# A router's products with the weights held in the array and the turned tokens moving, in a two-layer transformer kernel on one Trainium2 core

## Chip, cores and metric

The kernel runs on one core of a Trainium2 chip. The metric is the device time of one execution in microseconds (us). The core has a matrix engine (TensorE; PE in the profile, with its weight loads shown apart as PEld), a vector engine (DVE), a scalar engine (ACT), a general engine (POOL), and a queue processor (SP) that mainly issues transfers from memory. Each engine runs its own queue of instructions in order; engines wait for each other by semaphores.

## What is computed

The reference is a trunk of two layers over 512 latent tokens and 256 context tokens, 1024 channels wide. Each layer mixes tokens (layer 0 by a Fourier transform and a short gated convolution, layer 1 by windowed attention), adds the result to the stream, and then sends each token to two of 32 experts. The part that matters here is the step between the two: the residual sum, the normed and modulated row, and the router's logits.

```python
xl = xl + g1_l * yl
hl2 = modulate(rms_norm(xl, norm_ffn_g[layer]), sh2_l, sc2_l).reshape(B * L, D)
...
xr = xf.astype(jnp.float32)
g_logits = xr @ w_rg.astype(jnp.float32) + b_rg.astype(jnp.float32)
g_prob = jax.nn.softmax(g_logits, axis=-1)
g_val, g_idx = lax.top_k(g_prob, 1)
e_logits = (xr @ w_re.astype(jnp.float32) + b_re.astype(jnp.float32)).reshape(
    T, N_GROUPS, EXPERTS_PER_GROUP)
```

There are 4 group logits and 32 expert logits, so the router is a product of 1024 channels by 36 columns for each token. In layer 0 both streams pass through it (768 tokens, six tiles of 128), in layer 1 only the latent one (four tiles).

## The kernel before

`mixer_out` (line 1478) is the end of a layer's mixer and the start of its expert stage. It makes the mixer's output projection in two halves of 512 columns, `hf` = 0 and 1. For each half it goes over the token tiles `m`; the generator `tile(m)` issues for one tile 24 products into one accumulator `ps` (name A in the profile, two buffers): eight channel blocks `j` with three products each (L1540). Then DVE multiplies the accumulator by the gate (L1544) and adds it to the residual tile `x1[m]` (L1545). In the first half each `tile(m)` is run through at once.

In the second half, `x1[m]` is complete after L1545, and the generator `rows_and_logits` (line 174) does the rest for that tile. Its first step turns the tile, eight 128 x 128 transposes into two accumulators (L193), which ACT copies to `hT` (L194). ACT also squares the row and sums it (L201, then the root L160); DVE works out the scale `r` in small steps (L158 to L168). In layer 0, POOL multiplies the tile by its norm gain (L203), and DVE finishes the row (L218), which goes to memory for the expert stage's gather. In layer 1, ACT and DVE write the row as two parts (L208, L211) instead. The second step is the router: eight products in f32 with a block of `hT` (128 channels by 128 tokens) stationary and 36 columns of router weights `ws` moving (L223), and one DVE instruction that scales by `r` and adds the constant row (L224). `ws` is made once for each stream by `router(s)` (line 1485), as the router's weights times the modulation.

The steps of two tiles are interleaved by hand. Each pass `m` of the loop first issues four channel blocks of tile `m`, then the first step of tile `m - 1`, then the other four blocks and the update of tile `m`, then one step of any routing group under way, then the router of tile `m - 1`. `in_order` chains PE's and DVE's instructions in just this order, so neither engine can pass over one that waits. ACT, POOL and SP have an order that the compiler's own scheduler chooses.

Routing groups (`Route.tiles`, line 308) work on two tiles at a time (`CUTS`): after the logits of a group, DVE finds the top group and the two experts (L329 to L348), PE ranks the tokens (L356), DVE makes one-hot rows (L358 to L366), and PE counts the slots (L288). After the last tile, the group of the last two tiles ends the routing, and the expert stage (`moe`) begins: in layer 0 with a gather of rows (L764), in layer 1 with products on rows that are still on the core. Expert weights are loaded through a ring of eight buffers (L748); some of these buffers are those of the mixer's output weights and come free with the last L1540.

The accumulators of turning, router and ranking share one name, B, with three buffers taken in turn (`psB`). In the attention stage of layer 1, L2021 makes eight products in f32 with 64 stationary columns each, written to the upper and the lower half of the partitions by turns, with 128 columns moving.

Of the kernel before, what the change touches and what calls it, by code (L numbers as in the profile page):

```python
# [85 lines left out]
def body(tc, I, out, upto=None, dbg=None):  # L86
# [60 lines left out]
    epst = stat.tile([128, 1], F32, name="epst")  # L147
    V.memset(epst, EPS)
    rsq = stat.tile([128, 2, 4], F32, name="rsq")

    def slot(i, shape, dt=F32):

# [21 lines left out]
    def rows_and_logits(m, xm, hq, a2, b2, ws, crow, route, h2dst, wk, psum):  # L174
# [43 lines left out]
            V.scalar_tensor_tensor(h2, h2, r, b2, op0=ALU.mult, op1=ALU.add)  # L218
            route.wrote = (S if last else G).dma_start(h2dst[m * 128:(m + 1) * 128, :], h2)
        yield  # L220
        p = psum([128, 36])
        for k in range(8):
            T.matmul(p, hT[:, k, :], ws[:, k, :], start=k == 0, stop=k == 7)  # L223
        V.scalar_tensor_tensor(route.lg[:, m, :], p, r, crow, op0=ALU.mult, op1=ALU.add)  # L224
        yield

# [1251 lines left out]
    def mixer_out(layer, NT, lhs, raws, whls, x1, psA, psB, hq, rq, mk_route, h2dst, mdp, rw=None):  # L1478
# [6 lines left out]
        def router(s):  # L1485

            md = mds[s]
            V.scalar_tensor_tensor(md[:, 1, :], md[:, 1, :], 1.0, gf, op0=ALU.add, op1=ALU.mult)
            ws[s] = rq.tile([128, 8, 36], F32, name=f"ws{s}")
            V.tensor_mul(ws[s], wr, md[:, 1, :, None].to_broadcast([128, 8, 36]))  # L1490
            p = psB([128, 36])
            for k in range(8):
                T.matmul(p, md[:, 0, k:k + 1].to_broadcast([128, 128]), wr[:, k, :], start=k == 0, stop=k == 7)
            crow[s] = rq.tile([128, 36], F32, name=f"cr{s}")
            V.tensor_add(crow[s], p, br)
# [7 lines left out]
        for hf in range(2):  # L1503
# [6 lines left out]
            def tile(m):  # L1510
# [23 lines left out]
                        next(rl[m])  # L1534
                ps = psA([128, 512])
                for j in range(8):
                    if j == 4:
                        yield
                    for i, (a, b) in enumerate(((0, 0), (1, 0), (0, 1))):
                        T.matmul(ps, lhs(m, a, j), whl[b][:, j, :], start=j == 0 and i == 0, stop=j == 7 and i == 2)  # L1540
# [15 lines left out]
            for m in range(NT):  # L1556

                with in_order(*((PE, DVE) if m else (PE,)), chain=chain):
                    t = tile(m)
                    next(t)  # L1560
                    if m > 0:
                        next(rl[m - 1])
                    next(t)
                    going = [g for g in going if next(g, 0) is None]
                    if m > 0:
                        next(rl[m - 1])
                    for a, b in zip(cuts, cuts[1:]):
                        if b == m:
                            going.append(route.tiles(a, b))
                            next(going[-1])  # L1570
# [557 lines left out]
```

## Time and profile before

| | |
|---|---|
| time, median of 3 runs | 1613.04 us (1612.2 to 1615.1) |
| the profiled execution | 1612.01 us, span 1610.2 us |
| mean granted clock of TensorE in it | 0.98 |
| memory traffic over the span | 313 GB/s in the mean |
| layer 0's router (second half of `mixer_out`) | from about 266 to 320 us |
| layer 1's router | from about 1096 to 1130 us |

A time line of the profile gives the start of a group of instructions in us from the span's start, its length in us, the engine, the line of the kernel, the operation, the tile written and the tiles read, the shapes and the count. In square brackets stands how long the engine was idle before, and what ended that wait. A line of an answer for one source line gives the shortest, middle and longest duration in ns. PE's durations include the way through the array, so neighbouring instructions overlap; what a block of work takes is read from the start of its first weight load to the start of the next block's.

### The profile page before, as it was taken

To read this page: it belongs to the slowest core of one execution; us is meant where nothing else is said; L and a number is where in the kernel's file an instruction comes from. 1 tells how busy PE (TensorE), PEld (TensorE's weight loads), DVE (VectorE), ACT (ScalarE), POOL (GpSimd) and SP (SyncE) were. 2 spreads that over 40 slices of the span, in tenths; PEclk is the share of its full clock that TensorE was granted. 3 is DMA by queue.
4 is the path that set the end of the run, shared out by engine and by line. 5 is a ranking of instruction groups with operands and counts; after the bars stand their busy time and mean duration, and the time that the engine had idled before them with its cause. 6 is when DMAs were issued, how large, how long until landed. Compare 5 with 4: busy or idle time off the path is not lost. (4 is left out here: it accounts for less than half of the span.)

```text
span 1610.2 us, 21863 instructions
## 1 busy us (share of the span) xinstructions
PE 1511.0 (94%) x8201; PEld 865.1 (54%) x8201; DVE 749.6 (47%) x1688; ACT 437.1 (27%) x877; POOL 147.8 (9%) x169
## 2 busy tenths in 40 slices
PE   5999999999998999999989989999999999789887
PEld 3777888843443444444447776668443454334332
DVE  3555764973335334333466975645622233122223
ACT  4321320311111010111047577644221122112110
POOL 2612310300000000000033210000000000000000
PEclk9999999999999999999989999999999999899989
DMA  9889673879999999999930121025989999999996
GB/s 383 301 331 347 228 259 107 294 298 425 424 424 425 373 425 423 425 424 425 385 123 1 53 53 53 1 63 174 398 363 426 426 427 426 427 427 426 427 426 261
DMA packets 105889, 503.57 MB, mean 313 GB/s; under 512 B 15860, under 2 KB 30772, under 8 KB 53808
## 3 DMA queue, kind: packets, MB, share of 16 engines
q1 hardware_dynamic: 90256, 446.60, 68.7%
q0 software_dynamic: 12352, 52.31, 8.6%
q10 hardware_dynamic: 3168, 3.17, 0.6%
q8 instruction: 68, 1.11, 0.3%
q14 instruction: 45, 0.37, 0.1%
HBM read 499.30 MB, written 5.32 MB: 313 GB/s over the span
## 5 line engine op out<-in xcount | busy, mean ns | idle before, releaser
L913 PE MATMUL p<-w,xt 128*64 128x512 f32 (+1 forms) x1040 | 334.7, 603 | 15.8 <-DMA w<-in_w_dram 15.5
L913 PE MATMUL p<-r,xt 128*64 128x512 f32 (+1 forms) x784 | 278.8, 603 | 10.2 <-issue 6.3
L850 DVE TENSOR_TENSOR x<-x,cp 128x512 f32<-128x512 f32 x224 | 148.3, 686 | 98.9 <-PE cp L849 98.8
L930 DVE TENSOR_TENSOR sg<-sg,p 128x512 f32<-128x512 f32 x29 | 20.0, 688 | 342.8 <-PE p L913 332.7
L913 PEld LDWEIGHTS p<-w,xt 128*64 128x64 f32 (+1 forms) x1040 | 99.8, 133 | 147.2 <-issue 117.3
L849 PE MATMUL cp<-y,ot 128*128 128x512 f32 x600 | 168.1, 417 | 6.3 <-DVE x L850 3.8
L1000 PE MATMUL yp<-w,ht 128*64 128x512 f32 (+1 forms) x496 | 157.7, 595 | 2.6 <-DMA w<-in_w_dram 2.0
L913 PEld LDWEIGHTS p<-r,xt 128*64 128x64 f32 (+1 forms) x784 | 84.3, 135 | 134.7 <-issue 125.3
L1000 PE MATMUL yp<-r,ht 128*64 128x512 f32 (+1 forms) x368 | 129.1, 596 | 1.7 <-DMA r<-in_w_dram 1.7
L849 PEld LDWEIGHTS cp<-y,ot 128*128 128x128 f32 x600 | 104.4, 191 | 45.9 <-DVE x L850 24.2
L836 ACT CAST y<-yp 128x512 fp32r<-128x512 f32 x56 | 32.9, 587 | 286.7 <-DVE yp L827 200.2
L1000 PEld LDWEIGHTS yp<-r,ht 128*64 128x64 f32 (+1 forms) x368 | 37.6, 133 | 67.4 <-issue 63.3
L1000 PEld LDWEIGHTS yp<-w,ht 128*64 128x64 f32 (+1 forms) x496 | 45.7, 132 | 46.3 <-issue 40.2
L1951 DVE CUSTOM_DVE_ANT_0 A<-A,band,nsink 128x640 f32<-128x640 f32 (+1 forms) x56 | 45.3, 831 | 34.1 <-PE A L1947 33.9
L913 PE MATMUL p<-hhi,xt 128*64 128x512 f32 (+1 forms) x112 | 52.4, 613 | 6.5 <-DMA hhi<-in_w_dram 6.3
L920 ACT ACTIVATE sg<-p 128x512 f32<-128x512 f32 x29 | 17.3, 598 | 139.9 <-PE p L913 139.9
L825 DVE SCALAR_TENSOR_TENSOR sg<-yp,gsc,r 128x512 f32<-128x512 f32 x30 | 22.4, 747 | 69.8 <-PE yp L1000 69.7
L764 POOL DMA_INDIRECT r<-h_d,gi x17 | 17.0, 999 | 410.2 <-PE tp L799 290.3
L834 DVE SCALAR_TENSOR_TENSOR yp<-yp,gs,grow 128x512 f32<-128x512 f32 x24 | 18.2, 759 | 78.1 <-PE yp L1000 76.7
L913 PE MATMUL p<-hlo,xt 128*64 128x512 f32 (+1 forms) x112 | 51.2, 605 | 3.5 <-DMA hlo<-in_w_dram 3.5
L1947 PEld LDWEIGHTS A<-kS,w 128*128 128x128 f32 x288 | 36.1, 188 | 24.7 <-ACT w L1997 12.7
L1953 ACT ACTIVATE P<-A,nm 128x640 f32<-128x640 f32 (+1 forms) x56 | 42.5, 759 | 25.4 <-DVE nm L1951 25.4
(558 smaller groups left out, 2680.8 us busy)
## 6 DMA issues: line engine op xcount, KB each, us to landing
w<-in_w_dram SPq DMA_DIRECT2D x190, 1024.0 KB, 19.5
r<-in_w_dram SPq DMA_DIRECT2D x144, 1024.0 KB, 19.4
w<-in_w_mod_dram POOLq DMA_DIRECT2D x12, 2048.0 KB, 9.8
hhi<-in_w_dram SPq DMA_DIRECT2D x23, 1024.0 KB, 19.6
hlo<-in_w_dram SPq DMA_DIRECT2D x23, 1024.0 KB, 19.6
mw<-in_w_mod_dram POOLq DMA_DIRECT2D x32, 512.0 KB, 6.9
w<-in_w_in_even_dram SPq DMA_DIRECT2D x13, 512.0 KB, 7.4
w<-in_w_mod_dram SPq DMA_DIRECT2D x3, 2048.0 KB, 12.4
```

The source lines that it names most:

```text
L825: V.scalar_tensor_tensor(yc, ys, near["gsc"][:, j:j + 1], near["grow"][1][:, hs], op0=ALU.mult, op1=ALU.mult)
L834: V.scalar_tensor_tensor(ys, ys, tb["gs"][:, j:j + 1], near["grow"][0][:, hs], op0=ALU.mult, op1=ALU.mult)
L836: hi = S.copy(Yr[j, hf][0], ys)
L849: T.matmul(p, ot if len(Yr[j, hf]) > 1 else ot.bitcast(F32), y, start=n == 0 and i == 0, stop=n == len(js) - 1 and y is Yr[j, hf][-1])
L850: return V.tensor_add(xs, xs, p)
L913: T.matmul(ps[rs], X[b][:, q, rs], W[j, wn, ab][:, q, :], start=q == 0, stop=q == 7)
L920: si = S.activation(H[b], ps[:, cs], AF.Silu)
L930: V.tensor_mul(H[b], H[b], P1[b])
L1000: T.matmul(py_[hf][rs, :], HT[b][:, q, rs], W[j, "w2", ab][:, q, hf * 512:hf * 512 + 512], start=q == 0, stop=q == 3)
L1947: T.matmul(ps[:, o0:o0 + w], qS[G_][:, c, b * 128:(b + 1) * 128], kS[part][:, 2 * G_ + c // 4, k0:k0 + w], start=part == 0, stop=part == 1)
L1951: V.tensor_tensor_reduce(out=ps[:, 0:w], in0=ps[:, 0:w], in1=bnd, op0=ALU.add, op1=ALU.min, scale=1.0, scalar=nsink[:, hd:hd + 1], accum_o ...
L1953: S.activation(P[:, 0:w], ps[:, 0:w], AF.Exp, bias=nm[:, c:c + 1], scale=-1.0, accum_out=ls[:, c:c + 1])
```

## The change

For every tile but the last of a layer, the router's products swap their operands: a block of 64 router columns (36 and 28 zeros) is stationary, and the 128 turned tokens move. Even channel blocks write the lower half of an accumulator of 128 partitions, odd ones the upper half. ACT copies that accumulator to `lt`, and one more product, with `lt` stationary and a matrix `fold` of two stacked unit blocks moving, adds the two halves and turns the result back to tokens by 36 columns. L224 then reads it as before. The last tile keeps the old products.

The order changes too. `tile(m)` of the second half pauses before channel blocks 3 and 5 instead of before 4, and `rows_and_logits` has one step more. A pass now issues three channel blocks, the first step of tile `m - 1`, two blocks, the new router and its copy, three blocks and the update, the routing group's step, and then the fold and L224.

```diff
+    fold = stat.tile([128, 64], F32, name="fold")[:, 0:36]
+    V.tensor_add(fold, ident[:, 0:36], ident[:, 64:100])
...
         yield
-        p = psum([128, 36])
-        for k in range(8):
-            T.matmul(p, hT[:, k, :], ws[:, k, :], start=k == 0, stop=k == 7)
+        if last:
+            p = psum([128, 36])
+            for k in range(8):
+                T.matmul(p, hT[:, k, :], ws[:, k, 0:36], start=k == 0, stop=k == 7)
+        else:
+
+            p = psum([128, 128])
+            for k in range(8):
+                a = k % 2 * 64
+                T.matmul(p[a:a + 64], ws[:, k, :], hT[:, k, :], start=k < 2, stop=k > 5)
+            lt = wk.tile([128, 128], F32, name="lt")
+            S.copy(lt, p)
+            yield
+            p = psum([128, 36])
+            T.matmul(p, lt, fold, start=True, stop=True)
         V.scalar_tensor_tensor(route.lg[:, m, :], p, r, crow, op0=ALU.mult, op1=ALU.add)
         yield
...
-            ws[s] = rq.tile([128, 8, 36], F32, name=f"ws{s}")
-            V.tensor_mul(ws[s], wr, md[:, 1, :, None].to_broadcast([128, 8, 36]))
+            ws[s] = rq.tile([128, 8, 64], F32, name=f"ws{s}")
+            G.memset(ws[s][:, :, 36:64], 0.0)
+            V.tensor_mul(ws[s][:, :, 0:36], wr, md[:, 1, :, None].to_broadcast([128, 8, 36]))
...
                 for j in range(8):
-                    if j == 4:
+                    if hf and j in (3, 5):
                         yield
...
                     t = tile(m)
+                    next(t)
+                    if m > 0:
+                        next(rl[m - 1])
                     next(t)
                     if m > 0:
                         next(rl[m - 1])
```

## The prediction

> **What bounds the kernel now.** I read the page first, then the answers for the old router line and for the nearest row to its new form, then the weight loads and all engines in order of time around both routers, then stretches of the span.
>
> ```profile
> span 1610.2 us, 21863 instructions
> PE 1511.0 (94%) x8201; PEld 865.1 (54%) x8201; DVE 749.6 (47%) x1688; ACT 437.1 (27%) x877; POOL 147.8 (9%) x169
> ```
> ```profile
> 288.30:314.60 26.30, 25.44 (x160) 21.62 (x159) 24.93 (x75) 7.85 (x17) 11.72 (x9) 1.00 0.79 269
> 316.00:322.00 6.00, 6.00 (x36) 5.26 (x36) 4.92 (x24) 2.08 (x5) 0.00 (x0) 0.50 1.02 393
> 324.50:330.00 5.50, 5.25 (x57) 4.40 (x55) 5.00 (x33) 0.28 (x2) 1.09 (x1) 1.00 0.01 5
> 345.00:765.00 420.00, 411.73 (x2072) 180.75 (x2070) 167.57 (x315) 50.97 (x90) 14.88 (x15) 0.99 1.00 420
> 1210.00:1590.00 380.00, 343.53 (x1792) 151.62 (x1785) 96.91 (x157) 72.57 (x152) 0.00 (x0) 0.97 1.01 425
> ```
>
> The page says 94% PE, but that is a mean over stages. The second fence gives stretches: length, then busy time of PE, PEld, DVE, ACT and POOL, the clock, the DMA share, GB/s. The two long stretches (the experts) are bound by DMA, at 420 and 425 GB/s. Just before the first one DMA moves 5 GB/s: it waits for the routing. So a router that ends earlier or later moves what follows by as much. In layer 0's router (288.30 to 314.60) PE is busy for 25.44 us of 26.30, but DVE for 24.93: both are full, and the question is which of them ends last.
>
> **What an edit costs on PE.**
>
> ```profile
> L223 PEld LDWEIGHTS B<-ws,hT x160: 186/192/338, 278.0 to 1129.7; 128*128 128x128 f32 x160
> ```
> ```profile
> 274.31 1.10 PEld L193 LDWEIGHTS B<-cst,x 128*128 128x128 f32 x8
> 275.32 2.62 PEld L1540 LDWEIGHTS A<-r,r 128*128 128x128 f32 x12
> 277.98 1.98 PEld L223 LDWEIGHTS B<-ws,hT 128*128 128x128 f32 x16
> 279.88 2.60 PEld L1540 LDWEIGHTS A<-r,r 128*128 128x128 f32 x12
> ...
> 286.19 1.98 PEld L223 LDWEIGHTS B<-ws,hT 128*128 128x128 f32 x16
> ...
> 966.47 0.85 PEld L2021 LDWEIGHTS B<-cst,es 128*64 128x64 f32 x16 [0.17 <-issue]
> 967.50 0.77 PEld L1947 LDWEIGHTS A<-kS,w 128*128 128x128 f32 x6 [0.17 <-ACT w L1997]
> ```
>
> From start to start, which leaves no overlap to be counted twice: the turn of a tile (L193) takes 275.32 - 274.31 = 1.01 us, twelve products of L1540 (four channel blocks) 277.98 - 275.32 = 2.66, so one block 0.665; a tile's router 279.88 - 277.98 = 1.90. That router is 16 weight loads for eight products (160 over ten tiles), so one product costs 0.24. Its new form, 64 stationary columns in alternating halves with 128 columns moving in f32, is what L2021 already does with 16 loads: 967.50 - 966.47 = 1.03, or 1.20 with the 0.17 that stood idle before it. I take 1.03. The fold is one product of the old form, 0.24. A tile's period on PE therefore goes from 8 x 0.665 + 1.01 + 1.90 = 8.23 (the rows give 286.19 - 277.98 = 8.21) to 5.32 + 1.01 + 1.03 + 0.24 = 7.60. It saves **0.63** a tile, 5.0 for the five tiles of layer 0 and the three of layer 1.
>
> [...]
>
> **What the order costs, layer 0.** The new router comes before the last three channel blocks of the next tile, so these end 5.32 + 1.01 + 1.03 = 7.36 after the period's start, where they ended 5.32 + 1.01 = 6.33 after it. Only they release the residual update L1544 and L1545, and all of DVE's later work is queued behind it.
>
> ```profile
> 286.61 0.70 DVE L1544 TENSOR_TENSOR A<-A,gr 128x512 f32<-128x512 f32 x1 [0.94 <-PE A L1540]
> 287.35 0.69 DVE L1545 TENSOR_TENSOR x<-x,A 128x512 f32<-128x512 f32 x1
> ...
> 288.32 0.25 DVE L224 SCALAR_TENSOR_TENSOR w<-B,rq,cr 128x36 f32<-128x36 f32 x1 [0.29 <-PE B L223]
> ...
> 289.30 2.39 POOL L203 TENSOR_TENSOR h<-x,a 128x1024 f32<-128x1024 f32 x1 [2.76 <-ACT h L201]
> ...
> 289.59 2.13 DVE L337 TENSOR_TENSOR w<-w 128x8 f32<-128x8 f32 x1
> ...
> 297.41 1.06 ACT L201 ACTIVATE h<-x 128x1024 f32<-128x1024 f32 x1 [4.72 <-DVE x L1545]
> ...
> 298.81 2.37 DVE L366 TENSOR_TENSOR w<-w 128x32 bf16<-128x32 bf16 x1
> ...
> 301.10 0.24 DVE L224 SCALAR_TENSOR_TENSOR w<-B,rq,cr 128x36 f32<-128x36 f32 x1
> ...
> 304.11 0.69 DVE L1544 TENSOR_TENSOR A<-A,gr 128x512 f32<-128x512 f32 x1
> ...
> 313.88 0.69 DVE L1545 TENSOR_TENSOR x<-x,A 128x512 f32<-128x512 f32 x1
> ...
> 314.64 1.17 PEld L193 LDWEIGHTS B<-cst,x 128*128 128x128 f32 x8 [1.02 <-PE B L223]
> 316.41 3.49 PEld L223 LDWEIGHTS B<-ws,hT 128*128 128x128 f32 x16
> ```
>
> Tile 1's products start at 274.31 - 2.66 = 271.65. Tile 2's blocks ended at 286.19, when the router started; now they end at 271.65 + 7.60 + 7.36 = 286.61, **0.42 later**: one saving is behind them, one earlier router is ahead. L1544 followed PE by 0.42 and does so again. The 0.29 wait of L224 goes, since the fold is done by 286.9; but a DVE operation of 64 elements (L337) stands still until POOL's multiplication, which starts from the updated tile, ends at 289.30 + 2.39. That end moves by 0.42 too, so the 0.29 is lost again in that stall. From there to 314.57 DVE has no room: what PE saves on tiles 2 to 4 buys nothing, and the last tile's turn, which today waits 1.02 for its update, waits longer.
>
> One more wait is added. The tile B has three buffers, taken in turn; with the fold's accumulator the order is turn, turn, router, (rank), fold, and the router's buffer is always that of the fold before it, which L224 must have read. For tile 3 its turn waits for the tile's update, at 297.4 + 0.4, then 1.01 and two blocks, 1.33: PE is at the router at 300.1. L224 of tile 2 ends at 301.10 + 0.24 + 0.42 = 301.8. Behind the waiting router stand the three blocks: router to 302.8, blocks to 304.8, L1544 at 305.2 where it was 304.11. So from here DVE is **1.1 later**, not 0.42. If the buffer doesn't bind, 0.42 stays, and if L337 falls clear of POOL, 0.1. Layer 0: +1.1 (0.1 to 1.6).
>
> **Layer 1.** Here DVE has room, and PE sets the end.
>
> ```profile
> 1104.22 1.09 PEld L193 LDWEIGHTS B<-cst,x 128*128 128x128 f32 x8
> 1104.48 1.28 ACT L160 ACT_TABLE_LOAD   x1
> 1105.97 1.05 ACT L194 COPY hT<-B 128x512 f32<-128x512 f32 x2
> ...
> 1113.82 1.16 ACT L208 ACTIVATE x<-x,rq 128x1024 fp32r<-128x1024 f32 x1
> ...
> 1124.70 1.86 PEld L223 LDWEIGHTS B<-ws,hT 128*128 128x128 f32 x16
> 1124.83 0.70 DVE L1544 TENSOR_TENSOR A<-A,gr 128x512 f32<-128x512 f32 x1 [2.08 <-PE A L1540]
> 1125.57 0.69 DVE L1545 TENSOR_TENSOR x<-x,A 128x512 f32<-128x512 f32 x1
> 1126.40 1.09 PEld L193 LDWEIGHTS B<-cst,x 128*128 128x128 f32 x8
> ```
>
> Tile 1 starts at 1104.22 - 2.66 = 1101.56. The last tile's blocks ended by 1124.70; without waits they would end at 1101.56 + 2 x 7.60 + 7.36 = 1124.12, 0.5 earlier. But the turned tile is copied late: ACT loads a table first and its two copies run from 1105.97 to 1107.02, so half of it is there at 1106.5, and the moved router is ready at 1101.56 + 2.00 + 1.01 + 1.33 = 1105.90. That is 0.6 lost, and the end is 1124.7. If ACT copies first, the table and L208 come 1.05 later, and with them the update queued behind L211: as much, or up to 0.3 more. Then L1544 and L1545 take 0.2 + 1.43, so the last update ends at 1126.3 to 1126.6, today at 1125.57 + 0.69 = 1126.26. The 1.90 of router that covered it is down to 0.24 of fold: the saving of the last tile is spent on waiting, and DVE's work behind the update is 0.1 to 0.4 later. I take **+0.3** (-0.5 to +1.5: the lower end with no wait for ACT, the upper if L208's 1.16 falls between two copies, as it does today in tile 1).
>
> **The rest.** Copying lt takes ACT 0.2 to 0.6 (half a 1.05 pair is 512 columns; this has 128). Three blocks, 2.0 us, hide it; uncovered it would cost up to 0.6 a tile. The zeroing of 28 columns (POOL) and the one DVE addition at the start lie far ahead of any use: from nothing to the 0.25 of a L224, taken as nothing. No DMA is added; larger tiles shift SBUF places, whose waits no row shows: -1 to +1, taken as nothing. The first half's yield that goes changes no order, as that pass is run through.
>
> **Sum.** +1.1 + 0.3 = +1.4. The profiled execution took 1612.01 (span 1610.2 and 1.8 around it), so 1613.4 by it; the median of the runs shown is 1.0 higher, and on it the forecast is **1614.4**, +0.09%. About 0.2%, 3.2 us, is what a measurement of this kernel can tell from no change.
>
> **Rivals.**
> - PE's saving passes whole: 1613.0 - 5.0 = 1608.0. For it: PE is full in both routers. Against: DVE's 24.93 of 26.30, and the update that now comes behind the router. 0.18; a part of it, 1611.5, 0.07.
> - The clock. In layer 0 PE stands 1.02 us, turns a tile, and at 316.00 the clock is 0.50: the last router takes 3.49 instead of 1.98, 1.5 more. In layer 1 the new order opens a gap of 1.4 before the last turn. If the clock falls there too, its last router pays the same 1.5: 1615.9. 0.15. [...]
> - Slower: ACT's queue has the copy of lt behind the next tile's squares (L201). Those start when the update is done, 0.4 + 1.4 after the blocks' end, and take 1.06; copy and all, the fold and PE behind it wait some 3.4 us. It decides from one such tile in layer 1 on: 1614.4 + 3.4 = 1617.8; on all eight some 20 more. Against it: the router ends 2.0 before the blocks, so its copy is ready first. 0.10.
> - The forecast, 0.50, with -0.5 to +3.0 of its own (1612.5 to 1616.0).
>
> Faster comes to 0.20 (the first rival and a little of its part), slower to 0.18 (the third, a third of the clock's, the forecast's upper edge), no change to 0.62. The range leaves out the first rival and more than one tile of the third: 1609.5 to 1618.0.
>
> **What would show it.** Right: a new router of about 1.03 start to start; DVE as full as before up to the last update of layer 0, at 314 to 316; a gap over 2 us before the last turn there; router of tile 3 starting just after L224. Wrong: the last turn of layer 0 before 314, or layer 1's before 1126 after both stretches are aligned at tile 1; ACT's copy of lt behind L201; a clock under 1.00 in layer 1's router.

## The result, and the profile after

The changed kernel takes 1623.16 us (median of five runs, 1621.04 to 1625.11), the kernel before 1612.2 beside it: 1.0059 times as long, 95% interval 1.0046 to 1.0072, or some 9.5 us more by this ratio (the two medians are 11.0 us apart, the two profiled spans 11.1). The forecast was 1.4 us more, with 1618.0 as the upper end of its range. The profiled execution took 1623.09.

First the page of the changed kernel, then its answer for stretches that hold the same work as four of those shown of before (layer 0's router, its tail, the two expert stages); columns as there.

```profile
span 1621.3 us, 21922 instructions
PE 1513.0 (93%) x8217; PEld 863.6 (53%) x8217; DVE 751.3 (46%) x1689; ACT 438.1 (27%) x885; POOL 148.6 (9%) x172
```
```profile
288.70:316.20 27.50, 23.57 (x162) 18.16 (x160) 25.43 (x76) 8.64 (x21) 11.68 (x9) 1.00 0.72 253
317.40:323.40 6.00, 6.00 (x37) 5.18 (x37) 5.29 (x26) 2.15 (x5) 0.00 (x0) 0.57 1.02 372
347.00:767.50 420.50, 411.45 (x2070) 181.28 (x2066) 167.09 (x313) 50.90 (x90) 14.82 (x15) 0.99 1.00 418
1221.00:1601.00 380.00, 342.29 (x1790) 151.35 (x1784) 96.95 (x157) 72.41 (x152) 0.00 (x0) 0.98 1.01 425
```

In layer 0's router PE has 23.57 us of work where it had 25.44, DVE 25.43 where it had 24.93, and the stretch is 1.2 us longer: the saving on PE is there and buys nothing, as forecast. Now the time line of the changed kernel in the two routers.

```profile
301.52 0.24 DVE L238 SCALAR_TENSOR_TENSOR w<-B,rq,cr 128x36 f32<-128x36 f32 x1
301.91 1.09 PE L232 MATMUL B<-hT,ws 128*64 128x128 f32 x16 [1.27 <-DVE rr L165]
302.93 1.91 PEld L1555 LDWEIGHTS A<-r,r 128*128 128x128 f32 x9 [0.17 <-issue]
305.31 0.70 DVE L1559 TENSOR_TENSOR A<-A,gr 128x512 f32<-128x512 f32 x1 [0.72 <-PE A L1555]
...
316.15 1.33 PE L195 MATMUL B<-cst,x 128*128 128x128 f32 x8 [2.17 <-issue]
317.82 3.30 PE L226 MATMUL B<-ws,hT 128*128 128x36 f32 x16
...
1114.98 0.42 PEld L232 LDWEIGHTS B<-hT,ws 128*64 128x64 f32 x8 [0.56 <-ACT hT L196]
...
1133.82 0.70 DVE L1559 TENSOR_TENSOR A<-A,gr 128x512 f32<-128x512 f32 x1 [2.14 <-PE A L1555]
1135.36 1.12 PEld L195 LDWEIGHTS B<-cst,x 128*128 128x128 f32 x8 [1.37 <-issue]
...
1137.00 3.15 PEld L226 LDWEIGHTS B<-ws,hT 128*128 128x128 f32 x16
```

Layer 0 went step for step as forecast: the router of tile 3 waits for the sum of tile 2 (L238, which ends at 301.76; the bracket names L165, which ended last beside it) and starts at 301.9 (301.8 was forecast), and the last router starts at 317.82 where it started at 316.41. In layer 1 the forecast gap before the last turn is there (1.37), and behind it the router takes 3.15 us for the 1.86 of before: the clock fell (0.50 in the second line below), which the prediction had as a rival. The first line is the block that comes next.

```profile
804.00:806.00 2.00, 2.00 (x5) 1.51 (x6) 0.69 (x1) 0.00 (x0) 0.00 (x0) 0.50 0.47 142
1140.00:1142.00 2.00, 2.00 (x11) 1.45 (x11) 1.63 (x13) 0.00 (x0) 0.00 (x0) 0.50 1.02 422
```

The two routers together lose some 5 us. Most of the rest is lost in two places whose code the change doesn't touch. Both are shown by the time lines of the two kernels: first the end of the overflow block of layer 0, which every engine skips by a branch (L580, now L594), then the last block of layer 1's attention weights, which SP issues (L1772, now L1790), ACT rounds in eight pieces (L1642, now L1660) and which the turned queries (L1908, now L1926) wait for behind ACT and POOL. Before:

```profile
798.02 0.69 DVE L930 TENSOR_TENSOR sg<-sg,p 128x512 f32<-128x512 f32 x1 [10.11 <-PEq L580]
799.07 1.18 PE L849 MATMUL cp<-y,ot 128*128 128x512 f32 x4 [1.15 <-DVEq L580]
...
889.08 0.57 SPq L1772 DMA_DIRECT2D w<-in_w_qkv_dram  x1
897.47 4.27 ACT L1642 CAST w<-w 128x512 fp32r<-128x512 f32 x8 [3.84 <-DMA w<-in_w_qkv_dram]
904.23 1.42 PE L1908 MATMUL B<-cst,x 128*128 128x128 f32 x8 [0.54 <-POOL x L1819]
```

After:

```profile
800.74 0.69 DVE L944 TENSOR_TENSOR sg<-sg,p 128x512 f32<-128x512 f32 x1 [10.11 <-PE p L927]
803.98 2.04 PE L863 MATMUL cp<-y,ot 128*128 128x512 f32 x4 [3.33 <-PEq L594]
...
895.35 0.57 SPq L1790 DMA_DIRECT2D w<-in_w_qkv_dram  x1
904.84 4.27 ACT L1660 CAST w<-w 128x512 fp32r<-128x512 f32 x8 [4.94 <-DMA w<-in_w_qkv_dram]
911.58 1.44 PE L1926 MATMUL B<-cst,x 128*128 128x128 f32 x8 [1.63 <-POOL x L1837]
```

At the block PE stands for 3.33 us in place of 1.15, and its next four products take 2.04 in place of 1.18, at half clock (0.50 from 804 to 806). ACT's first piece starts 9.49 us after the issue of the weights in place of 8.39, and the turned queries wait 1.1 us longer.

### The profile page after: what moved, and what is told of

It is laid out like the page before. It is cut to its first block, busy times and chain, and to the rows that moved or that the text cites. A ratio compares the mean times of both kernels' runs of the same rounds, so it can differ in the third digit from the quotient of the medians.

```text
span 1621.3 us, 21922 instructions
## 1 busy us (share of the span) xinstructions
PE 1513.0 (93%) x8217; PEld 863.6 (53%) x8217; DVE 751.3 (46%) x1689; ACT 438.1 (27%) x885; POOL 148.6 (9%) x172
## 4 chain that ended last, share of the span: by engine, by line
PE 32%; DMA 12%; DVE 3%; ACT 3%; issue 1%; SPq 0%; ACTq 0%; DVEq 0%
PE p L927 8%; DMA w<-in_w_dram 6%; DMA hlo<-in_w_dram 5%; PE yp L1014 4%; PE cp L863 3%; PE A L1847 3%; PE tp L806 2%; PE A L1965 2%; PE O L2027 2%; PE B L2012 2%; PE A L1555 2%; DMA w<-in_w_qkv_dram 1%; DMA w<-in_w_o_dram 1%; ACT P L1971 1%; PE tp L813 0%
## 5 line engine op out<-in xcount | busy, mean ns | idle before, releaser
L818 ACT COPY xt<-tp 128x512 f32<-128x512 f32 x34 | 18.4, 589 | 115.0 <-PE tp L813 114.9
```

## The experiments

Each was run beside the kernel before, with three or five rounds. The table has for each kernel the ratio to the kernel before with its interval, the place T of the end of the skipped block among PE's instructions (modulo 256; how it is counted stands in the expectation of shift_before), PE's idle time there, the time from the issue of those attention weights to ACT's first use, and then how much later than in the kernel before an instruction of DVE starts, in us. That is taken from the two time lines, instruction by instruction; the columns are named by the time in the kernel before, and each is the middle value of the instructions within 6 us of it.

```
                ratio  interval         T  idle load   278   304   540   768   815   846   952  1110  1150   end
before          1                     187  1.15 8.39
after           1.0059 1.0046-1.0072  211  3.33 9.49  -0.0   1.2   1.9   2.7   6.0   5.9   7.9   8.7  11.5  11.3
pad_before      1.0041 1.0026-1.0057  207  3.35 9.26   1.0   1.0   2.9   2.9   5.5   4.3   8.9   8.9   8.9   8.9
pad_after       1.0024 1.0010-1.0037  191  1.15 8.31   1.1   2.3   3.3   3.2   5.6   5.9   6.0   6.8   7.2   6.9
products        1.0034 1.0021-1.0048  210  3.31 9.44   0.5   0.6   1.3   2.0   5.2   5.1   7.2   7.2   8.3   7.9
old_products    1.0041 1.0025-1.0056  189  1.15 8.17   1.2   5.6   7.6   7.6   7.8   8.1   7.2   8.4   9.4   9.0
shift_before    1.0041 1.0029-1.0053  212  3.35 9.23  -0.5  -0.5   1.2   2.5   3.6   2.5   4.1   4.0   4.0   4.1
mid_before      1.0053 1.0033-1.0073   94  1.15 7.98   5.0   5.0   5.4   5.3   4.3   6.5   8.2   8.3   8.4   8.3
mid_after       1.0068 1.0045-1.0090   92  1.15 8.18   6.8   8.0  11.5  11.7  10.7  10.8  13.1  14.0  16.9  16.5
warm1           1.0064 1.0041-1.0086  211  3.39 9.76   0.4   1.6   2.6   3.5   6.8   6.7  10.5  11.9  12.3  12.1
clear_before    0.9999 0.9988-1.0010   41  3.34 8.38   0.2   0.2  -0.0  -0.1   2.3   0.2  -0.2  -0.3  -0.3  -0.4
clear_after     1.0043 1.0029-1.0057   49  3.32 8.32   1.7   2.9   5.0   4.9   7.5   6.4   7.2   8.0  10.9  10.5
clear_products  1.0020 1.0008-1.0032   48  3.30 8.09   2.9   3.0   4.2   4.2   7.4   7.4   7.1   7.1   7.4   7.0
one_bank        1.0061 1.0046-1.0076  210  3.44 9.28   0.6   1.8   2.4   3.5   6.7   4.8   5.1   5.7   8.6   8.4
late_before     1.0018 1.0007-1.0029  187  1.16 9.35  -0.7  -0.7   1.4   2.2   2.0   2.7   3.0   2.9   2.9   2.8
mid_after2      1.0033 1.0020-1.0047   95  1.15 8.23   1.4   2.6   3.2   3.4   2.5   4.4   6.5   8.3   8.7   8.4
mid_warm2       1.0032 1.0021-1.0042   95  1.15 8.15   0.3   1.5   2.1   2.0   1.0   3.3   5.4   7.2   7.7   7.5
mid_products    1.0024 1.0014-1.0034   94  1.15 7.99   2.8   2.9   2.2   2.4   1.4   2.3   3.9   4.1   4.5   4.2
far_fold        1.0143 1.0126-1.0160  214  3.37 9.29  -0.0   6.7   5.8   5.8   9.2   9.1  11.0  12.2  18.3  18.0
far_warm        1.0108 1.0089-1.0126   98  1.15 8.02   1.9   8.6  11.1  11.3  10.3  12.2  14.1  17.3  22.5  22.0
```

A row is one execution, and executions of one kernel differ by some us: the ten of shift_before lie between 1616.14 and 1623.64, and its row is the fastest of them. Steps that many rows share are therefore read from the table, totals from the ratios.

### What the products cost, what the order, what the length of the code

The changed kernel executes eight more products, the folds (16 in the profile's count, five of the eight in layer 0), so its instructions behind layer 0's router stand later in the code. The first four runs separate this from the products and from the order. pad_before and pad_after change only the idle products behind the last rank of layer 0 (128 x 256, bfloat16; in the kernel before 45, from 326.22 to 331.31, at a clock of 1.00), ten more in the kernel before and ten fewer in the changed one:

```diff
-                idle(45 if self.spill else 5, self.psum)
+                idle(55 if self.spill else 5, self.psum)    (pad_before)
+                idle(35 if self.spill else 5, self.psum)    (pad_after)
```

> The kernel before with ten more filler products (55 instead of 45) at the end of layer 0's routing, in a stretch in which PE waits for the first gather; the routers are untouched. In code length on PE this equals the five folds that the change adds in layer 0, and the compiler's order of ACT and PE in the early attention stage comes out as in the changed kernel. Theory 'elsewhere' (about half of the changed kernel's 11 us does not come from the routers but from where PE's code lies at the branch near 799 us and from the attention stage's order): +4 to +6 us over before, with PE standing some 4 us at that branch instead of 2. Theory 'routers only': within 1 us of before.

> The changed kernel with ten filler products fewer (35 instead of 45) at the end of layer 0's routing, so that PE's code is as long up to the branch near 799 us as in the kernel before. Theory 'elsewhere': 4 to 6 us faster than the changed kernel, +5 to +7 over before, all of it in the two routers. Theory 'routers only': as the changed kernel, +11, or more if PE's clock falls in the shorter filler stretch.

products has the new products with the old order, and old_products the old products with the new order (the pause stands before the router instead of behind it):

```diff
 products, against the changed kernel
-            yield
             p = psum([128, 36])
...
-                    if hf and j in (3, 5):
+                    if hf and j == 4:
...
-                    next(t)
-                    if m > 0:
-                        next(rl[m - 1])
 old_products, against the changed kernel: the products of the kernel before, and
+        if not last:
+            yield
```

> The new products and the fold, but in the old order: router, copy and fold at the end of a pass, after the update. Theory 'order' (the routers lose by the router that moved ahead of the update and by the gap before the last turn, not by the new products): both routers end within 0.7 us of before, no clock under 1.00 in layer 1's router. With 'elsewhere' the branch still costs 2 to 3 us, since the code is as long as in the changed kernel, while the attention order is nearly that of before: +2 to +3.5 in all. [...]

> The old products, no copy and no fold, in the new order (router after five blocks, its read by DVE at the end of the pass). Theory 'order': layer 0's last turn is 1.5 to 4 us late, layer 1's last turn is late too with a gap before it and a clock of 0.50 in its last router, and the branch near 799 us is as in before, since the code is no longer: +4 to +8 in all. If the new products are the cost: as before, within 1 us.

Ten idle products in the kernel before, whose result nobody reads, cost 1.0041, and they bring both foreign losses: 3.35 us idle at the block, 9.26 us for the weights. (In these four kernels the compiler also orders a few of ACT's instructions in the attention stage anew, so they don't yet tell order from place.) Ten fewer in the changed kernel take both away. The new products alone, in the old order, have both too; old_products, two instructions longer than the kernel before, has neither, and loses 4.4 us in layer 0's router instead (from 278 to 304). So the order alone costs more than it does with the new products, the products cost little in the routers (0.15 there), and the length of PE's code costs something of its own. Two expectations failed here. products costs 5.5 us by its ratio, not 2 to 3.5, and its clock fell in layer 1's last router all the same, behind an idle time of PE of 0.37; old_products kept its clock there, behind a gap of 1.60. A stretch of products, and the weight loads of old_products:

```profile
1137.00:1139.00 2.00, 2.00 (x11) 1.62 (x12) 1.09 (x9) 0.35 (x1) 0.00 (x0) 0.50 0.99 418
```
```profile
1135.71 1.12 PEld L195 LDWEIGHTS B<-cst,x 128*128 128x128 f32 x8 [1.60 <-issue]
1136.96 0.38 PEld L292 LDWEIGHTS <-y 128*64 128x64 bf16 x8
1137.35 1.86 PEld L225 LDWEIGHTS B<-ws,hT 128*128 128x128 f32 x16
```

The two kernels that went on after 1.15 us stood still again a little later, at places that differ: old_products behind three products, pad_after behind two. The time line of old_products, then that of pad_after:

```profile
806.66 0.93 PE L853 MATMUL cp<-y,ot 128*128 128x512 f32 x3 [1.15 <-DVEq L584]
808.58 0.51 PE L853 MATMUL cp<-y,ot 128*128 128x512 f32 x1 [1.00 <-issue]
```
```profile
802.30 0.69 PE L863 MATMUL cp<-y,ot 128*128 128x512 f32 x2 [1.15 <-DVEq L594]
804.22 1.22 PE L863 MATMUL cp<-y,ot 128*128 128x512 f32 x2 [1.23 <-DVE x L864]
```

Each such product is two instructions, so old_products met its obstacle 6 instructions behind the block's end at T = 189, and pad_after 4 behind T = 191: both at 195. pad_before, products and the changed kernel, at 207 to 211, are past it when the block ends.

### Only the place of the code

Small products at the very start, where PE waits for its first input, move all of PE's code and nothing else; warm1 is about layer 1's clock.

```diff
+    pn = psM()
+    for _ in range(12):        (shift_before; 82 in mid_before, 70 in mid_after)
+        T.matmul(pn[:, 0:64], tri, ident.bitcast(BF)[:, 0:64], start=True, stop=True)
     for m in range(6):
         xt = xts[m]
```
```diff
 warm1, against the changed kernel, ahead of the last turn
+                if layer:
+                    idle(10, psA)
                 next(rl[m])
```

> The kernel before, with 12 small products (64 columns each) put in where TensorE waits for its first input, ahead of everything; nothing else is changed. Two theories for the 3 us that the change loses at the skipped overflow block. POSITION: what decides is where the block's end lies in TensorE's instructions. Counted in the built programs (a float32 product 4 instructions, a turn or a float32r product 2, a bfloat16 product 2, a wait 1; so counted, the executed products are 8201 before and 8217 after, as the profiles have them), that place stands at 187 (modulo 256) in the kernel before, at 189 and 191 in the two runs whose TensorE went on within 1.2 us and then stood still 3 and 2 products later, and at 207, 210 and 211 in the three that stood still 3.3 us at the block's end itself. All six fit a border of 256 instructions at 195. The 12 products bring it to 212: TensorE idle 3.3 us there in place of 1.15, granted clock about 0.5 in the 4 us behind, 2.5 to 3.5 us later at the first product of the next stage, and about 1617 to 1619 against 1614 to 1615. ORDER: the loss came with the router's new order or with its products: here then nothing, within 1 us of the kernel before.

> The control of the run above: the same small products at the same place, but 82 of them, so that the end of the skipped block stands at 94 (modulo 256), in the middle between two borders. POSITION: TensorE goes on 1.15 us after the block as before, clock 1.00; within 1 us of the kernel before, perhaps 0.5 faster. If the products at the start cost something by themselves, or if any shift of the code costs, it is 2 us or more slower like the run above.

> The changed kernel with 70 such small products at the start, which puts the end of the skipped block at 92 (modulo 256). POSITION: the idle time of 3.33 us at the block goes back to 1.15 and the clock stays at 1.00 there; 3 us less than the changed kernel, 1619 to 1621 where the kernel before takes 1614.5; if the 2 us lost between 850 and 950 hang on the same thing, 1617 to 1618. ORDER: no gain, 1623.

> The changed kernel with ten idle products (128 x 256, bfloat16, like those that the rank has) ahead of the last turn of layer 1, in the gap of 1.4 us in which TensorE waits for the last tile's update. CLOCK: the gap with the turns behind it is what brings the granted clock to 0.50 between 1138 and 1144; filled, the clock stays at 0.9 or more, the last router takes 1.9 us in place of 3.15, and the kernel is 2 to 3 us faster than the changed one, some 1620.5. If the clock falls for the router's own alternating halves, it falls here too and the time stays at 1623, or the ten products add 0.5.

The time line of shift_before:

```profile
803.71 1.17 PE L849 MATMUL cp<-y,ot 128*128 128x512 f32 x4 [3.35 <-PEq L580]
```

Twelve products 800 us earlier give the 3.35 us, and 1.0041: the idle time at the block hangs on the place of PE's code alone. In this execution the clock held (the four products take 1.17), so the loss at 815 is 1.2 us and not 3. mid_before and mid_after are clear of the block (1.15), as expected, but as times both miss: their 82 and 70 products take 4.5 and 3.9 us, and the compiler orders the start anew around them, at 5 to 7 us by 278. warm1 does at its place what it should. Its time line, and its answer for the stretch behind:

```profile
1138.60 1.29 PE L195 MATMUL B<-cst,x 128*128 128x128 f32 x8 [0.19 <-DVE x L1560]
1140.21 1.98 PE L226 MATMUL B<-ws,hT 128*128 128x36 f32 x16
```
```profile
1137.00:1147.00 10.00, 9.08 (x89) 7.74 (x86) 8.22 (x43) 3.13 (x6) 0.00 (x0) 1.00 0.92 359
```

The clock stays at 1.00, and from 1110 to 1150 it loses 0.5 us where the changed kernel loses 2.9. So the router's alternating halves alone don't bring the clock down. That the gap does is not shown: pad_after, and mid_after2 below, have the same gap with nothing in it and kept the clock as well (each loses 0.5 from 1110 to 1150), as old_products did, and products lost it without such a gap. And the median is no better than the changed kernel's (1.0064), so what the clock costs a typical run is not shown either.

### A kernel clear of the border

To keep the start as it is, the next runs lengthen the code in the idle products behind the rank, whose order is fixed by hand: half the columns, twice as many. one_bank is about layer 0's wait.

```diff
-    def idle(n, psum):
+    def idle(n, psum, c=256):
...
-            T.matmul(p, tri, ident.bitcast(BF), start=True, stop=True)
+            T.matmul(p[:, 0:c], tri, ident.bitcast(BF)[:, 0:c], start=True, stop=True)
...
-                idle(45 if self.spill else 5, self.psum)
+                idle(*((92, self.psum, 128) if self.spill else (5, self.psum)))
 clear_products and clear_after have 92, clear_before 100; mid_after2, mid_warm2, mid_products 115
```
```diff
 one_bank, against the changed kernel
-            p = psum([128, 128])
+            pq = psum([128, 164])
...
-            p = psum([128, 36])
+            p = pq[:, 128:164]
```

> The new products in the old order, as in the run of the products alone (1618.6 there, ratio 1.0034); the 45 idle products of 256 columns at the end of layer 0's rank are 92 of 128 columns, the same time of TensorE but 94 instructions more, so that the end of the skipped overflow block stands at 48 (modulo 256), clear of the border at 195, in place of 210. No other engine's order changes. BORDER: TensorE idle 1.15 us at the block in place of 3.31 and no half clock there; some 6 us less, since the shift alone cost 1.0041 in the kernel before: 1612 to 1615 where the kernel before takes 1613.5, ratio 0.998 to 1.001. If the products themselves cost the time: ratio 1.003 again.

> The changed kernel with the same edit (end of the block at 49 in place of 211). If border and order add up: the border's 6 us go, and the order's 3 to 4 stay (1.0024 in the run with ten idle products fewer, which stood just ahead of the border): ratio 1.002 to 1.003, 1617 to 1618. If all of the loss hung on the border: ratio 1.000. If the order alone makes it: 1.006 again.

> The kernel before with 100 idle products of 128 columns in place of 45 of 256 (end of the block at 41 in place of 187): the control for the two runs above. Within 1 us of the kernel before: the edit costs nothing by itself. If 100 short products last longer than 45 long ones and delay the rank's lists, up to 1 us more, seen at 319 to 326.

> The changed kernel with the fold's result in the bank that the products wrote (columns 128 to 163), so that a tile takes one of the three buffers B less; same instructions, same places of the code to within one wait. BUFFER: in layer 0 the router of tile 3 no longer waits for the sum of tile 2 (idle 1.68 us ahead of its weight load, start 301.88); it starts some 1 us earlier, the last router of the layer 1 us earlier, and the kernel is 1 us faster than the changed one, 1622 (1.0052 to 1.0055). If VectorE's full row sets the layer instead, the wait moves elsewhere and nothing changes.

All three clear kernels stood still 3.3 us at the block all the same: the expected place of "clear" was wrong. With the border at 195, T is 102 to 110 behind it in these, 12 to 19 in the others that stood still, and 153 to 159, or 248 to 252, in those that didn't. One reading of these counts fits all: the jump costs only the 1.15 us if it ends in the block of 256 instructions that follows the one it starts in, and 3.3 if it goes one further. With a skipped block of L instructions it goes one further when T lies less than L - 256 behind the border, so L is between 367 and 409 (356 were counted, so the count misses at least eleven).

The traces show such blocks. The page of the changed kernel lists transfers of instructions (fetches), 16384 bytes each, beside the others (packets, MB, share of 16 engines):

```profile
q8 instruction: 68, 1.11, 0.3%
```

and the trace has their times (start in us, duration). Between the fourteen of them from 411.82 to 749.76 in the kernel before PE starts 3329 weight loads and products, 256.1 from one to the next. All of PE's, 2 x 8217, alone fill 64 blocks of 256, so that 68 fits PE's code with its waits. In the kernel before PE goes on at 799.07, while the fetch of 798.55 still runs; in the changed kernel it goes on at 803.98, 1.8 us after the fetch of 801.11 has ended. That it has the block's end already in the one and waits for it in the other is the author's reading of these times.

```
              at the branch                   near the attention weights
before        798.55 (1.00), 802.09 (1.12)    896.60 (0.92)
after         801.11 (1.03), 804.34 (0.93)    900.79 (0.92)
late_before   800.68 (1.01), 804.07 (0.88)    896.44 (0.92)
```

clear_before shows the second thing: with 3.34 us idle at the block it is as fast as the kernel before. In its row the 2.3 us lost there are won back by 846, and nothing is lost behind. So in this kernel the idle time at the block costs nothing by itself. What it does not have is the late load, and neither have the two others: clear_after is 0.0016 below the changed kernel, clear_products 0.0014 below products, with the same idle time at the block (in both pairs the intervals overlap). And one_bank left its wait where it was, 1.27 us:

```profile
302.47 1.09 PE L232 MATMUL B<-hT,ws 128*64 128x128 f32 x16 [1.27 <-DVE rr L165]
```

The router of tile 3 now takes the very buffer of tile 2, which the same sum frees, so this run couldn't tell the theories apart.

### The load and the fetch, and the change without them

late_before moves only the code behind the skipped block; the others have 115 short idle products.

```diff
 late_before, against the kernel before, behind the first turned rows of layer 1
+        pn = mps.tile([128, 512], F32, name="cp", bufs=2)
+        for _ in range(12):
+            T.matmul(pn[:, 0:64], tri, ident.bitcast(BF)[:, 0:64], start=True, stop=True)
         for m in range(4, 6):
```

> The kernel before, with 12 small products (64 columns, some 0.7 us of TensorE) behind the skipped block, where TensorE then waits 2.67 us for the last turned rows; no other engine's order changes. In the fourteen profiles so far the last block of w_qkv (issued by SP at 889 in the kernel before, awaited by ScalarE's eight casts ahead of the queries) lands 9.23 to 9.76 us after its issue in the six kernels whose TensorE passes a border of 256 of its instructions 6.8 to 7.4 us after the issue, and 7.98 to 8.39 us in the eight others. FETCH: the load of TensorE's next instructions shares the DMA engines with the weights. The 12 products move the border from 8.7 to some 7 us after the issue and leave the block's end where it is: 1.15 us idle at the block, the load 9.2 to 9.5 us in place of 8.4, TensorE's wait ahead of the first turned queries 1.3 us in place of 0.54; 0.8 us later behind it, or 2.4 where the clock falls for it; 1.0005 to 1.002. If the slower load came from the lost time at the block or from the order, it is 8.4 us here and the ratio 1.000.

> The changed kernel with 115 idle products of 128 columns in place of 45 of 256 in layer 0's rank, so that the end of the skipped block stands at 95 (modulo 256), as in the one run that was clear of it (94: idle 1.15 us); no other engine's order changes. The three runs at 41 to 49 stood still 3.3 us all the same, so the border rule holds only if the skipped block is longer than the 356 instructions counted, by 9 to 55. POSITION: idle 1.15 us and clock 1.00 at the block, the load of w_qkv 8.0 to 8.4 us. What is left is the order: 1.2 us in layer 0's router, 0.8 in layer 1's first tiles and 2.9 with the half clock of its last router (four of five runs of this order had it): ratio 1.0025 to 1.0035 in place of 1.0059. If position is not the cause, 1.005 to 1.006.

> The same with the ten idle products ahead of layer 1's last turn. In the run that had them alone the clock stayed at 1.00 there and this stretch cost 0.5 us in place of 2.9, though the whole kernel was no faster (1.0064). Here 2 us less than the run without them: ratio 1.001 to 1.002. If the ten products only move the loss elsewhere: the same ratio as that run.

> The new products in the old order with the 115 idle products (end of the block at 94). Stretch by stretch the products by themselves cost 0.15 us in layer 0's router and 0.2 to 1.1 in layer 1's; without the two losses by position: ratio 0.9995 to 1.001, against 1.0034 and 1.002 in the two runs that stood still at the block. If the products cost more than these stretches show, 1.002 again.

The time line of late_before:

```profile
891.05 0.57 SPq L1775 DMA_DIRECT2D w<-in_w_qkv_dram  x1
900.40 4.27 ACT L1642 CAST w<-w 128x512 fp32r<-128x512 f32 x8 [4.78 <-DMA w<-in_w_qkv_dram]
907.14 1.44 PE L1911 MATMUL B<-cst,x 128*128 128x128 f32 x8 [1.46 <-POOL x L1822]
```

Twelve products behind the block turn 8.39 us into 9.35, and the turned queries wait 1.46 in place of 0.54, as expected; the block's end is untouched (1.16). Over all twenty kernels the load takes 9.23 to 9.76 us in the eight where PE crosses a border of 256 instructions 6.5 to 7.4 us after the issue, and 7.98 to 8.39 in the twelve others, with none in between. The fetch itself starts 5.2 to 5.7 us after the issue in the eight; in three of the others it starts 7.5 us after it, and in nine none falls into the load. The trace says why: in late_before the fetch (896.44, 0.92 us) falls into the middle of the load's packets (892.40 to 900.00), in the kernel before (896.60) into their last 0.6 us (890.43 to 897.18). In the changed kernel (fetch at 900.79) some 16 of the load's packets run at a time up to 902.25, and one at a time from 903.25 to the end at 904.44. A fetch that holds up a part of the load for as long as it lasts would do just this, as ACT waits for the whole; that it does so is the author's estimate. The ratio, 1.0018 (1.0007 to 1.0029), is at the upper end of what was expected, and of the size of the two differences above. That both losses together cost 1.0041 in the kernel before (shift_before), more than the one (clear_before, nothing) and the other (this run) by themselves, was not followed further.

In mid_after2 both places are as in the kernel before (1.15 and 8.23), with the changed kernel's order on all other engines, and the ratio falls from 1.0059 to 1.0033: the place of the code is some 4 us of the 9.5, though the two intervals overlap a little. mid_warm2 gains nothing over it (1.0032): its clock at the last router stays up, but in mid_after2's execution it did so too, from 1110 to 1150 both lose 0.5. mid_products misses: 1.0024, not 1.000. The six kernels with T from 92 to 98 win 1 us at the block, and lose 2.4 to 4.4 us between 815 and 952. There DVE stands still in tiny operations while POOL works on the attention weights, as in the time line of mid_warm2:

```profile
823.11 4.75 DVE L1264 TENSOR_SCALAR A<-AB 128x16 f32<-128x16 f32 x1
828.84 1.22 PE L863 MATMUL cp<-y,ot 128*128 128x512 f32 x2 [4.87 <-DVE x L864]
```

In the kernel before, the same operation (L1250) took 0.24 us. It takes 0.92 to 4.75 in these six, 1.71 in old_products and 0.22 to 0.24 in the other thirteen. Here it ends when POOL's multiplications do, between 827.8 and 827.9:

```profile
820.35 7.48 POOL L1699 TENSOR_TENSOR w<-r,w 128x512 fp32r<-128x512 f32 x6
```

Set against DVE's row (the table's column 815), these multiplications end 2.0 to 3.3 us later in the six than in the kernel before, 0.2 later in old_products, and at the same time in the others. In five of the six (not in mid_before) SP also issues the first attention weights some 1.5 us later than its lag explains: in mid_after2 at 810.23, in the kernel before at 805.31, with 3.4 at 768; in the other fifteen the difference is below 0.2. So the six seem to have a loss of their own that is not the router's, and 1.0033 may hold a part of it. Why SP is late there, and whether POOL is the cause on DVE, was not tried.

### Layer 0's wait once more

The fold's result goes into the free half of the accumulator of the tile that is being added, so that it takes no buffer B; far_fold against the changed kernel, far_warm against mid_warm2.

```diff
-            p = psum([128, 36])
+            p = route.ps[:, 512:548]
             T.matmul(p, lt, fold, start=True, stop=True)
...
-                ps = psA([128, 512])
+                ps = psA([128, D])
+                if hf:
+                    route.ps = ps
+                ps = ps[:, 0:512]
```

> The changed kernel with the fold's result in the free half of the accumulator of the tile that is being added (the second bank of its A), so that the fold takes no buffer B and the router of a tile takes a buffer that ScalarE's copy has freed long before. The run with the fold in the products' own bank left the wait as it was: idle 1.27 us ahead of the router of tile 3, behind the sum of tile 2 on VectorE, and 1.21 us lost between 278 and 304, the same as in the changed kernel. BUFFER: here the router of tile 3 starts when its turned rows are copied, some 1 us sooner after the products ahead of it (0.2 us in place of 1.27), and the stretch from 278 to 304 loses 0 to 0.5 us; the rest as in the changed kernel, ratio 1.005 to 1.0055. VECTOR: the row of VectorE sets the layer whatever TensorE waits for: 1.2 us again.

> The same edit in the kernel that is clear at the block, at the weight load and of layer 1's half clock (1.0032): the changed kernel with all that the runs so far point to. BUFFER: 1 us less, ratio 1.002 to 1.0025. VECTOR: 1.003. In neither is it faster than the kernel before.

Neither theory's number came. The time line of far_fold:

```profile
300.39 0.38 PE L237 MATMUL A<-fold,lt 128*128 128x36 f32 x2 [1.67 <-DVE x L1563]
...
306.71 1.09 PE L232 MATMUL B<-hT,ws 128*64 128x128 f32 x16
```

The router of tile 3 waits for nothing any more, so the wait of 1.27 us was one for the buffer. But in its place PE waits 1.4 to 1.7 us at every fold (7.9 us over the five tiles) for an update on DVE, and this layer loses 6.7 us. What the buffer's wait alone costs the layer stays open.

## Why the prediction was wrong

**PE's saving: right in kind, mis-sized, and without effect.** The new router takes 1.03 us from start to start, as forecast, and the fold less than its 0.24 (0.14 from 286.93 to the next start at 287.07). But a period is 7.86 us (routers at 275.88 and 283.74) where the old one was 8.21, and not 7.60: a tile saves 0.35, not 0.63. By PE's starts in one period the old router takes 1.70 (286.42 to 288.12), the new one and its fold 1.17; and the mixer's 24 products, cut in three, take 5.89 where they took 5.71, with 0.17 of idle time ahead of the weight load behind each router. The parts priced from one pair of starts each add up to the old period, but not in the new arrangement. With the 1.20 that the prediction had beside the 1.03, a tile would save 0.46, which was nearer. The trace has a stop of 0.17 behind each new router, with no cause that it shows; of the 0.35 or 0.36 idle ahead of one, the 0.35 at 283.74 is put down to ACT's copy.

**Layer 0: right.** +1.1 was forecast. From 278 to 304 the changed order loses 1.2 in each of the eight rows that have the new order with the new products and the fold in a buffer B, and 1.5 us are there at the first expert product (335.80 after 334.27). That DVE is full and takes up PE's saving, the wait for the sum of tile 2 and its time (301.8) came as written.

**Layer 1: the mechanism right, the size short.** The copy behind ACT's table load held up the router as forecast (0.56 idle at 1114.98); with the longer period the last update ends 1.1 us later, not 0.3: 1134.56 + 0.69, which is 1127.39 in the time of before, when tile 1's updates (1109.71 and 1101.85) are laid on each other. **The clock** was a rival at 0.15 and 1.5 us. It fell in the profiled execution and in three of the five others with the new order and products and nothing in the gap (2.9 against 0.5 us from 1110 to 1150; far_fold left out), and in products, which has the old order, so the chance was too low; but no median shows its cost.

**The step that failed** is the sum: it added the two routers and took all that follows as unchanged. "No DMA is added; larger tiles shift SBUF places ... taken as nothing" looked for foreign costs in the wrong store. Eight more products shift PE's code, which comes in by transfers of its own (16384 bytes to 256.1 weight loads and products). With the shift PE stood 3.33 us in place of 1.15 at the end of a jump, and a fetch fell into the middle of a weight load that PE waits for (9.49 us in place of 8.39): with the order unchanged, 12 products at the start of the kernel before cost 1.0041 in this way (shift_before), the load alone 1.0018 (late_before), and the jump alone nothing (clear_before). The prediction had no term for it, and no rival. By mid_after2, which has neither, this is some 4 us of the 9.5, about half of the 8 us by which the forecast is short; layer 1's size is 0.8 of the rest, and what remains is not explained.

What stays open: with both places clear the change still costs 1.0033, some 5.3 us, of which the two routers show 2.6 (1.2 from 278 to 304, 0.9 from 1049 to 1110, 0.5 from there to 1150, in mid_after2). The rest lies mostly between 815 and 952, where the kernel before seems to stand well, and where mid_products, with the old order, loses 2.5 too. No version came out faster than the kernel before; the nearest is clear_before, 0.9999 (0.9988 to 1.0010).

## What to carry to other kernels

In a kernel tuned to 0.2%, a change can have a price outside its own stage, as here some 4 us of the 9.5: count how many instructions it adds to an engine, and look at what comes later that hangs on their place, the ends of skipped blocks first, then transfers that the engine waits for with nothing to spare. Test it with a few idle instructions in the unchanged kernel: if they cost about as much as the change does, its own work is not the whole cause. And take the price of a block of work from the starts of its products as well as from those of its weight loads: for the old router they gave 1.70 and 1.90.

## What the runs showed of the hardware

- At the end of the skipped block TensorE stood idle 1.15 or 1.16 us in ten kernels, and 3.30 to 3.44 in ten. By the author's count (367 to 409 instructions skipped, the bounds worked out above) the jump ends in the next block of 256 in the first ten, and one block further in the others.
- The transfers of TensorE's instructions have 16384 bytes each, 256.1 weight loads and products apart from 412 to 750 us in the kernel before. A weight load that has one of 0.92 us in its middle is about 1 us later: 9.23 to 9.76 us from issue to use in eight kernels, 7.98 to 8.39 in twelve.
- The granted clock is 1.00 or 0.50 in the traces of the kernel before and the changed one from 19 us on, and each stretch at 0.50 that ends within the span lasts 3.41, 6.83 or 10.24 us: in the kernel before 6.83 from 315.87 (layer 0's last router) and 3.41 from 838.10, in the changed kernel 6.83 from 1137.41 (layer 1's last router). What makes it fall is not shown: with the same gap ahead of layer 1's last turn it was 0.50 behind it in the changed kernel and stayed up in pad_after and mid_after2.
